# A mixture-of-experts kernel whose first piece of x is loaded ahead of the hand-synchronized section, which GpSimd enters at once and closes itself

## The chip, the cores and the metric

The kernel runs on one core of a Trainium2 chip. The metric is the device time of one execution, in microseconds; a number is the median of several runs. Besides the time, each run can leave a profile of one execution: every instruction of every engine with start and duration, the semaphore updates, and every DMA packet. The profile counts its span from the first to the last instruction of the program; the device time is longer, because it also has what lies outside the program's own instructions.

The engines are called here as the profile calls them: PE (TensorE, matrix products), PEld (its weight loads), DVE (VectorE), ACT (ScalarE), POOL (GpSimd) and SP (SyncE). A small q behind the name (SPq) means an instruction that only the engine's sequencer carries out.

## The reference

Eight experts each take 256 rows of 512 numbers through two matrix products with a ReLU in between:

```python
# x: 8 x 256 x 512, w1: 8 x 512 x 2048, w2: 8 x 2048 x 512, all float32
h = np.matmul(x, w1)
h = np.maximum(h, 0)
return np.matmul(h, w2).astype(np.float32)
```

Each weight is used for the 256 rows of one expert and never again. The weights are 2 x 33.6 MB of float32, and x and the result are 4.2 MB each.

## The kernel before

The kernel computes in bf16. Weights are read from memory as float32 and turned into bf16 by the DMA transfer itself; such casting transfers are issued by POOL, and they all stand in one queue. Each weight transfer holds one matrix of one expert (the last w2 comes in two halves) and fills one of four slots for w1 or for w2.

x goes another way at its start. Its first quarter (HEAD = 4 of 16 blocks) is loaded as float32 by SP's own queue into `x_head` and cast by DVE; POOL loads the other three quarters with the casting transfer. Both land in the third w2 slot, which is free until then. PE transposes x from there, with `identity` as the second operand, and ACT and DVE copy the transposed x from PSUM into `xT`.

Everything stands inside a critical section of Tile: in it the kernel places its own waits, and Tile only brings all engines into it and out of it again. The parts that the change touches:

```python
d_head, d_x = sem("d_head"), sem("d_x")
d_first, d_out, d_last = sem("d_first"), sem("d_out"), sem("d_last")
s_zero, s_ident, s_cast = sem("s_zero"), sem("s_ident"), sem("s_cast")
...
d_w = [sem(f"d_w{i}") for i in range(len(loads))]        # 17, one for each weight transfer

with tc.tile_critical(no_gpsimd_drain=True):             # SP is the section's own engine

    sp.dma_start(x_head[:], x_v[:, :HEAD * H]).then_inc(d_head, 16)
    for i, (w, e, h, n) in enumerate(loads):
        sp.wait_ge(d_w[i], 16)                           # a weight has landed: tell PE
        sp.sem_inc(c_w1, 1)                              # (or c_w2)
    sp.wait_ge(v_last, MC)
    sp.dma_start(out_v[:, E - 1, :], ...).then_inc(d_last, 16)   # result of the last expert

    pool.dma_start(x_sb[:, HEAD * H:], x_v[:, HEAD * H:]).then_inc(d_x, 16)
    pool.wait_ge(s_zero, 1)                              # DVE has zeroed identity
    pool.affine_select(out=identity[:], ...).then_inc(s_ident)
    for i, (w, e, h, n) in enumerate(loads):
        ...                                              # waits until the slot is free
        pool.dma_start(dst, src).then_inc(d_w[i], 16)
    pool.wait_ge(v_out, 2)
    pool.wait_ge(d_first, 16)
    pool.dma_start(out_v[:, :E - 1, :], ...).then_inc(d_out, 16) # results of experts 0 to 6
    pool.drain()

    dve.memset(identity[:], 0.0).then_inc(s_zero)
    ...
    dve.wait_ge(d_head, 16)
    dve.tensor_copy(x_sb[:, :HEAD * H], x_head[:]).then_inc(s_cast)
    ...                                                  # copies of xT and of results

    ...                                                  # ACT: copies of xT, ReLU of h
    act.wait_ge(d_out, 16)
    act.wait_ge(d_last, 16)

    pe.wait_ge(s_ident, 1)
    pe.wait_ge(s_cast, 1)
    pe.wait_ge(d_x, 16)
    loop("transposes", count, K1, transposes)
    ...
    loop("expert", count, E, expert)                     # h = x w1 by halves, then o = h w2
```

In an expert, PE waits for that expert's w1 (`c_w1`), makes h in four groups of 32 products, and then waits for w2 (`c_w2`) and makes the result.

Of the kernel before, what the change touches and what calls it, by code (L numbers as in the profile page):

```python
# [7 lines left out]

FP32 = mybir.dt.float32
BF16 = mybir.dt.bfloat16  # L10
PE = mybir.EngineType.PE

FIRST_FREE = 16512


@with_exitstack
def kernel(
# [7 lines left out]
    nc = tc.nc  # L25
    P = 128
    E, C, H = x.shape
# [7 lines left out]
    HEAD = 4  # L35

    NS = 4
# [11 lines left out]
    x_v = x.rearrange("e (pp r) k -> (e pp) (r k)", r=R)  # L49
# [4 lines left out]

    places, free = {}, FIRST_FREE

    def allot(name, shape, dtype):
        nonlocal free
        places[name] = free
        t = nc.alloc_sbuf_tensor_at(name, shape, dtype, offset=free)  # L60
        free += math.prod(shape[1:]) * mybir.dt.size(dtype)
        return t
# [3 lines left out]
    xT = allot("xT", [P, K1, MC, E * P], BF16)  # L66
    hT = allot("hT", [P, K2, C], BF16)
    out_sb = allot("out_sb", [P, E, MC, H], FP32)
    x_head = allot("x_head", [P, HEAD * H], FP32)
    identity = allot("identity", [P, P], BF16)  # L70
    W1_AT, W2_AT, XT_AT = places["w1_sb"], places["w2_sb"], places["xT"]

    x_sb = w2_sb[:, 2, :]
# [6 lines left out]
    def sem(name):  # L80
        return tc.alloc_semaphore(name)


    d_head, d_x = sem("d_head"), sem("d_x")
    d_first, d_out, d_last = sem("d_first"), sem("d_out"), sem("d_last")

    s_zero, s_ident, s_cast = sem("s_zero"), sem("s_ident"), sem("s_cast")
    p_xt, p_h, p_o = sem("p_xt"), sem("p_h"), sem("p_o")
    v_out, v_last = sem("v_out"), sem("v_last")

# [4 lines left out]
    loads = []  # L95
    for e in range(E - 1):
        loads += [(1, e, 0, 2), (2, e, 0, 2)]
    loads += [(1, E - 1, 0, 2), (2, E - 1, 0, 1), (2, E - 1, 1, 1)]
    d_w = [sem(f"d_w{i}") for i in range(len(loads))]

    with tc.tile_critical(no_gpsimd_drain=True):  # L101


        sp = nc.sync
        sp.dma_start(x_head[:], x_v[:, :HEAD * H]).then_inc(d_head, 16)
        for i, (w, e, h, n) in enumerate(loads):
            sp.wait_ge(d_w[i], 16)
            if w == 1:
                sp.sem_inc(c_w1, 1)
            else:  # L110
                sp.sem_inc(c_w2, n)
# [4 lines left out]


        pool = nc.gpsimd
        pool.dma_start(x_sb[:, HEAD * H:], x_v[:, HEAD * H:]).then_inc(d_x, 16)  # L119
        pool.wait_ge(s_zero, 1)  # L120

        pool.affine_select(  # L122
            out=identity[:],
# [7 lines left out]
        for i, (w, e, h, n) in enumerate(loads):  # L131


            old = e - NS
            if (w, e) == (2, 2):
                pool.wait_ge(p_xt, K1 * MC)
            if old >= 0 and h == 0:
                if w == 1:
                    pool.wait_ge(p_h, NG * (old + 1))
                else:  # L140
                    pool.wait_ge(p_o, MC * (old + 1))
            if i == len(loads) - 1:


                pool.wait_ge(v_out, 1)
                pool.dma_start(  # L146
                    out_v[:16, 0:5:2, :16], out_sb[:16, 0:5:2, 0, :16]
                ).then_inc(d_first, 16)
            if w == 2:
                src = w2_v[:, e, h:h + n, :].rearrange("p h n -> p (h n)")  # L150
                dst = w2_sb[:, e % NS, h * JH * H:(h + n) * JH * H]
            else:
                src, dst = w1_v[:, e, :], w1_sb[:, e % NS, :]
            pool.dma_start(dst, src).then_inc(d_w[i], 16)  # L154
        pool.wait_ge(v_out, 2)
        pool.wait_ge(d_first, 16)
        pool.dma_start(  # L157
            out_v[:, :E - 1, :], out_sb[:, :E - 1].rearrange("p e m h -> p e (m h)")
        ).then_inc(d_out, 16)
        pool.drain()  # L160

# [5 lines left out]


        dve = nc.vector
        dve.memset(identity[:], 0.0).then_inc(s_zero)  # L172
        dve.sem_inc(c_xt[0], 1)
        dve.sem_inc(c_o, MC)
        dve.wait_ge(d_head, 16)
        dve.tensor_copy(x_sb[:, :HEAD * H], x_head[:]).then_inc(s_cast)  # L176
        for ko in range(K1):
            dve.wait_ge(p_xt, ko * MC + 1)
            copy_xt(dve.tensor_copy, ko, 0).then_inc(c_xt[0])
# [11 lines left out]
        act = nc.scalar  # L191
# [14 lines left out]
                ).then_inc(c_h)  # L206
        act.wait_ge(p_o, E * MC)
        act.copy(out_sb[:, E - 1, 1, :], o_ps[1][:]).then_inc(v_last)  # L208
        act.wait_ge(d_out, 16)
        act.wait_ge(d_last, 16)  # L210

# [1 line left out]
        pe = nc.tensor  # L215
# [17 lines left out]
        def matmul(dst, weights, moving, **flags):  # L233
            inst = mybir.InstMatmult(
                name=nc.get_next_instruction_name(),
                engine=PE,
                ins=[moving, weights],
# [7 lines left out]
        def loop(name, counter, times, body):  # L245
            head, end = f"{name}_head", f"{name}_end"
            nc.br(head, engines=[PE])
            with nc.body(head, valid_engines=[PE]):
                body()
# [39 lines left out]
                    i += 1  # L289
                t.then_inc(p_xt)  # L290

        pe.wait_ge(s_ident, 1)
        pe.wait_ge(s_cast, 1)
        pe.wait_ge(d_x, 16)
        pe.reg_mov(count, 0)
        pe.reg_mov(reg["x"], X_AT + last_column(K1))
        loop("transposes", count, K1, transposes)
# [116 lines left out]
        loop("expert", count, E, expert)  # L414


# [1 line left out]
_INS = ['x', 'w1', 'w2']  # L418
_OUTS = [((8, 256, 512), 'float32')]
# [25 lines left out]
```

## Time and profile before

| what | before |
| --- | --- |
| device time, median of 3 runs | 181.04 us (181.02 to 181.25) |
| device time of the profiled run | 181.29 us |
| span of the profiled run | 179.5 us |
| PE busy | 130.4 us (73%) |
| ACT, DVE, POOL busy | 38.7, 15.9, 11.7 us |
| moved by DMA, as counted by packets | 40.37 MB, mean 225 GB/s |
| read from and written to memory | 71.30 MB and 4.20 MB |
| mean granted clock of PE | 0.961 |

The span is also shown in 40 equal slices, each about 4.5 us. A digit is a busy share in tenths, and the row DMA is the mean busy share of the core's 16 DMA engines. A stretch view gives the same for any stretch of time that is asked for: busy time of each engine, then the granted clock of PE, the busy share of the DMA engines and what they moved. A share slightly over 1 comes from packets that overlap on an engine. The timeline lists instructions by start and duration, and behind an instruction, in brackets, how long its engine had been idle and what ended that.

### The profile page before, as it was taken

What the parts mean: (1) busy time and instruction counts of PE and PEld (TensorE: products, weight loads), DVE (VectorE), ACT (ScalarE), POOL (GpSimd) and SP (SyncE); (2) the same over time, 40 slices, a digit from 0 to 9 for tenths busy, and PEclk for the clock granted to TensorE, in tenths of its full rate; (3) what the DMA queues carried; (4) which work ended last, traced back from release to release, by engine and by line L of the source; (5) the groups of instructions that cost most, each with busy time, mean ns of one, the idle gap of its engine ahead of it and who ended that gap; (6) DMA issues with size and microseconds to landing.
All of it is one profiled execution on the core that took longest, in us unless ns stands there. A gap on an engine that the chain in (4) does not pass through costs nothing. (4 is left out here: it accounts for less than half of the span.)

```text
span 179.5 us, 2103 instructions
## 1 busy us (share of the span) xinstructions
PE 130.4 (73%) x824; PEld 90.9 (51%) x832; DVE 15.9 (9%) x21; ACT 38.7 (22%) x38; POOL 11.7 (7%) x25
## 2 busy tenths in 40 slices
PE   0007659997949794949778698949894968769980
PEld 0007548746924493418633495428741963359630
DVE  0203420002000200020002000020002000200010
ACT  2002423500520044003500044003600350004410
POOL 7100030101010101010101000020000000002000
PEclk9999999999987999999999699996999999969999
DMA  5999999999999999999999999999999999999995
GB/s 186 261 203 226 230 208 204 234 215 197 230 226 212 204 230 215 197 234 226 193 223 230 208 204 234 215 197 230 226 212 204 230 215 201 230 201 211 351 423 217
DMA packets 3824, 40.37 MB, mean 225 GB/s; under 512 B 368, under 2 KB 368, under 8 KB 1392
## 3 DMA queue, kind: packets, MB, share of 16 engines
q0 software_dynamic: 3536, 38.80, 96.9%
q1 hardware_dynamic: 288, 1.57, 2.3%
HBM read 71.30 MB, written 4.20 MB: 421 GB/s over the span
## 5 line engine op out<-in xcount | busy, mean ns | idle before, releaser
L243 PE MATMUL h_ps<-xT,w_sb 128*128 x512 | 65.2, 292 | 17.1 <-PEq L218 17.1
L243 PEld LDWEIGHTS h_ps<-xT,w_sb 128*128 x512 | 59.5, 147 | 24.7 <-issue 21.7
L243 PE MATMUL o_ps<-w_sb,hT 128*128 x248 | 57.8, 387 | 11.0 <-PEq L218 10.6
L202 ACT ACTIVATE hT<-h_ps 128x1024 bf16<-128x1024 f32 x32 | 32.8, 1024 | 111.3 <-PE h_ps L243 111.3
L243 PEld LDWEIGHTS o_ps<-w_sb,hT 128*128 128x128 bf16 x256 | 24.9, 99 | 41.6 <-issue 14.0
L185 DVE COPY out_sb<-o_ps 128x512 f32<-128x512 f32 x15 | 9.7, 686 | 141.4 <-PE o_ps L243 141.4
L243 PE MATMUL xt_ps<-identity,w_sb 128*128 128x128 bf16 x64 | 7.6, 310 | 16.0 <-PEq L218 16.0
L243 PEld LDWEIGHTS xt_ps<-identity,w_sb 128*128 x64 | 6.5, 145 | 16.8 <-issue 16.8
L154 POOL DMA_DIRECT2D w_sb<-in_w_dram x17 | 9.1, 542 | 87.7 <-PE o_ps L243 34.5
L165 ACT COPY xT<-xt_ps 128x1024 bf16<-128x1024 bf16 x4 | 4.0, 1012 | 18.2 <-PE xt_ps L243 18.2
L165 DVE COPY xT<-xt_ps 128x1024 bf16<-128x1024 bf16 x4 | 4.9, 1224 | 11.9 <-PE xt_ps L243 11.9
L157 POOL DMA_DIRECT2D out_dram<-out_sb x1 | 0.9, 950 | 44.3 <-DMA out_dram<-out_sb 44.3
L208 ACT COPY out_sb<-o_ps 128x512 f32<-128x512 f32 x1 | 0.6, 586 | 5.9 <-PE o_ps L243 5.9
L146 POOL DMA_DIRECT2D out_dram<-out_sb x1 | 0.6, 557 | 20.0 <-DVEq L188 20.0
L176 DVE CAST w_sb<-x_head 128x2048 bf16<-128x2048 f32 x1 | 1.2, 1227 | 4.8 <-DMA x_head<-in_x_dram 4.8
L165 ACT ACT_TABLE_LOAD x1 | 1.3, 1283 | 1.1 <-SPq L101 1.1
L119 POOL DMA_DIRECT2D w_sb<-in_x_dram x1 | 0.7, 682 | 1.0 <-DVE identity L172 1.0
L122 POOL TENSOR_SCALAR_AFFINE_SELECT identity<-identity 128x128 bf16<-128x128 bf16 x1 | 0.3, 305 | 0.1
L172 DVE MEMSET identity<- 128x64 uint32 x1 | 0.1, 112 | 1.0 <-SPq L101 1.0
L429 POOL MEMSET const-float32-0.0<- 128x1 f32 x1 | 0.1, 99 | 0.2 <-issue 0.2
L429 POOL MEMSET const-bfloat16-1.0<- 128x1 bf16 x1 | 0.1, 102 | 0.0
L429 POOL MEMSET const-uint8-127<- 128x1 uint8 x1 | 0.1, 102 | 0.0
(1 smaller groups left out, 0.1 us busy)
## 6 DMA issues: line engine op xcount, KB each, us to landing
w_sb<-in_w_dram POOLq DMA_DIRECT2D x15, 2048.0 KB, 65.7
out_dram<-out_sb POOLq DMA_DIRECT2D x1, 3584.0 KB, 12.9
w_sb<-in_w_dram POOLq DMA_DIRECT2D x2, 1024.0 KB, 57.1
w_sb<-in_x_dram POOLq DMA_DIRECT2D x1, 1536.0 KB, 11.7
x_head<-in_x_dram SPq DMA_DIRECT2D x1, 1024.0 KB, 5.0
out_dram<-out_sb SPq DMA_DIRECT2D x1, 512.0 KB, 3.0
out_dram<-out_sb POOLq DMA_DIRECT2D x1, 3.0 KB, 44.8
```

Source lines behind the costliest of these rows:

```text
L119: pool.dma_start(x_sb[:, HEAD * H:], x_v[:, HEAD * H:]).then_inc(d_x, 16)
L122: pool.affine_select(out=identity[:], in_=identity[:], compare_op=mybir.AluOpType.not_equal, fill=1.0, base=0, pattern=[[-1, P]], channel_ ...
L146: pool.dma_start(out_v[:16, 0:5:2, :16], out_sb[:16, 0:5:2, 0, :16]).then_inc(d_first, 16)
L154: pool.dma_start(dst, src).then_inc(d_w[i], 16)
L157: pool.dma_start(out_v[:, :E - 1, :], out_sb[:, :E - 1].rearrange("p e m h -> p e (m h)")).then_inc(d_out, 16)
L165: return copy(xT[:, ko, m].rearrange("k (ep r2) -> k ep r2", r2=R // MC), xt_ps[m][:].rearrange("k r2 ep -> k ep r2"),)
L176: dve.tensor_copy(x_sb[:, :HEAD * H], x_head[:]).then_inc(s_cast)
L185: cp = dve.tensor_copy(out_sb[:, e, m, :], o_ps[m][:])
L202: act.activation(hT[:, g * GJ:(g + 1) * GJ, :].rearrange("p a c -> p (a c)"), h_ps[g % UG][:], mybir.ActivationFunctionType.Relu,).then_in ...
L208: act.copy(out_sb[:, E - 1, 1, :], o_ps[1][:]).then_inc(v_last)
L243: return pe.add_instruction(inst)
L429: nc = _bacc.Bacc("TRN2", target_bir_lowering=False, num_devices=1)
```

## The change

x_head becomes a tile of a Tile pool. Its load and its cast are moved ahead of the critical section, and Tile places the waits for them. The section is given POOL as its own engine, so that POOL takes no part in what the others wait for when they enter; only ahead of the transfer that overwrites x does it wait for Tile's data (`wait_critical_data_deps`). POOL also zeroes `identity` itself, and at the end it is POOL that waits for the two last transfers, in place of ACT. The weight transfers share one semaphore for each slot, counted up to 32, in place of one for each transfer; POOL's other transfers share one as well. The addresses of the large buffers move up by 8192 bytes a partition, since `x_head` now lies in front of them. The kernel allocates 13 semaphores fewer.

What it is for: SP and POOL are to issue the first transfers without waiting for each other, and fewer semaphores have to be cleared at the end.

```diff
-    with tc.tile_critical(no_gpsimd_drain=True):
+    landed = [
+        (d_half, 16) if h else ((d_w1, d_w2)[w - 1][e % NS], 16 * (e // NS + 1))
+        for w, e, h, _ in loads
+    ]
+    x_pool = ctx.enter_context(tc.tile_pool(name="x_pool", bufs=1))
+    x_head = x_pool.tile([P, HEAD * H], FP32, tag="x_head")
+    nc.sync.dma_start(x_head[:], x_v[:, :HEAD * H])
+    nc.vector.tensor_copy(x_sb[:, :HEAD * H], x_head[:])
+    with tc.tile_critical(sync_engine=POOL, no_gpsimd_drain=True):
...
-        sp.dma_start(x_head[:], x_v[:, :HEAD * H]).then_inc(d_head, 16)
         for i, (w, e, h, n) in enumerate(loads):
-            sp.wait_ge(d_w[i], 16)
+            sp.wait_ge(*landed[i])
...
-        pool.dma_start(x_sb[:, HEAD * H:], x_v[:, HEAD * H:]).then_inc(d_x, 16)
-        pool.wait_ge(s_zero, 1)
+        pool.dma_start(x_sb[:, HEAD * H:], x_v[:, HEAD * H:]).then_inc(d_pool, 16)
+        pool.memset(identity[:], 0.0).then_inc(s_ident)
+        pool.wait_ge(s_ident, 1)
...
             if (w, e) == (2, 2):
+                tc.wait_critical_data_deps()
                 pool.wait_ge(p_xt, K1 * MC)
...
-            pool.dma_start(dst, src).then_inc(d_w[i], 16)
+            pool.dma_start(dst, src).then_inc(landed[i][0], 16)
         pool.wait_ge(v_out, 2)
-        pool.wait_ge(d_first, 16)
+        pool.wait_ge(d_pool, 32)
         pool.dma_start(out_v[:, :E - 1, :], ...)     # the line is cut
-        ).then_inc(d_out, 16)
-        pool.drain()
+        ).then_inc(d_pool, 16)
...
-        dve.memset(identity[:], 0.0).then_inc(s_zero)
-        dve.wait_ge(d_head, 16)
-        dve.tensor_copy(x_sb[:, :HEAD * H], x_head[:]).then_inc(s_cast)
...
-        act.wait_ge(d_out, 16)
-        act.wait_ge(d_last, 16)
...
-        pe.wait_ge(s_ident, 1)
-        pe.wait_ge(s_cast, 1)
-        pe.wait_ge(d_x, 16)
+        pe.wait_ge(s_ident, 2)
+        pe.wait_ge(d_pool, 16)
...
+        pool.drain()
+        pool.wait_ge(d_pool, 48)
+        pool.wait_ge(d_last, 16).then_inc(s_ident)
```

The order in which the built program holds the instructions shows what Tile makes of it:

- SP's first instruction behind the opening barrier is now the transfer of `x_head`. Before, it was an empty instruction that raised a semaphore, and then a branch that waited for it; all engines had such a branch.
- POOL has an empty instruction in the same place, without a wait, and then its transfer of the other three quarters of x.
- SP, ACT and PE now enter the section only when the cast of x by DVE is done.
- At the end, before: all engines reported to SP, ACT after its two waits. After: POOL waits for the transfers and raises a semaphore, the other four engines answer it, and both POOL and SP wait for the answers, SP in three instructions more, before the closing barrier.
- The instruction that clears semaphores clears numbers 99 to 140 before, 42 in all, and 99 to 129 after, 31 in all, because Tile adds 8 of its own now and 6 before.

More of the change, by code (lines that the diff above doesn't have):

```diff
@@ L10 @@
 BF16 = mybir.dt.bfloat16
-PE = mybir.EngineType.PE
-FIRST_FREE = 16512
+PE, POOL = mybir.EngineType.PE, mybir.EngineType.Pool
+FIRST_FREE = 16512 + 8192
 @with_exitstack
@@ L68 @@
     out_sb = allot("out_sb", [P, E, MC, H], FP32)
-    x_head = allot("x_head", [P, HEAD * H], FP32)
     identity = allot("identity", [P, P], BF16)
@@ L81, in sem @@
         return tc.alloc_semaphore(name)
-    d_head, d_x = sem("d_head"), sem("d_x")
-    d_first, d_out, d_last = sem("d_first"), sem("d_out"), sem("d_last")
-    s_zero, s_ident, s_cast = sem("s_zero"), sem("s_ident"), sem("s_cast")
+    d_w1 = [sem(f"d_w1{i}") for i in range(NS)]
+    d_w2 = [sem(f"d_w2{i}") for i in range(NS)]
+    d_half, d_pool, d_last = sem("d_half"), sem("d_pool"), sem("d_last")
+    s_ident = sem("s_ident")
     p_xt, p_h, p_o = sem("p_xt"), sem("p_h"), sem("p_o")
@@ L98 @@
     loads += [(1, E - 1, 0, 2), (2, E - 1, 0, 1), (2, E - 1, 1, 1)]
-    d_w = [sem(f"d_w{i}") for i in range(len(loads))]
-    with tc.tile_critical(no_gpsimd_drain=True):
+    landed = [
[7 more added lines that the diff above has]
+    with tc.tile_critical(sync_engine=POOL, no_gpsimd_drain=True):
         sp = nc.sync
-        sp.dma_start(x_head[:], x_v[:, :HEAD * H]).then_inc(d_head, 16)
         for i, (w, e, h, n) in enumerate(loads):
-            sp.wait_ge(d_w[i], 16)
+            sp.wait_ge(*landed[i])
             if w == 1:
@@ L147 @@
                     out_v[:16, 0:5:2, :16], out_sb[:16, 0:5:2, 0, :16]
-                ).then_inc(d_first, 16)
+                ).then_inc(d_pool, 16)
             if w == 2:
@@ L153 @@
                 src, dst = w1_v[:, e, :], w1_sb[:, e % NS, :]
-            pool.dma_start(dst, src).then_inc(d_w[i], 16)
+            pool.dma_start(dst, src).then_inc(landed[i][0], 16)
         pool.wait_ge(v_out, 2)
-        pool.wait_ge(d_first, 16)
+        pool.wait_ge(d_pool, 32)
         pool.dma_start(
             out_v[:, :E - 1, :], out_sb[:, :E - 1].rearrange("p e m h -> p e (m h)")
-        ).then_inc(d_out, 16)
-        pool.drain()
+        ).then_inc(d_pool, 16)
         def copy_xt(copy, ko, m):
```

## The prediction, made before the changed kernel had run

> **What bounds the kernel now.** I read the slices first, because PE is busy for only 73% of the span and something else must fill it. Then I read stretches cut where the DMA row changes, then the timeline of the first 12 us, and last the chain of waits, to see whether its answer agrees.
>
> From the page:
>
> ```profile
> DMA  5999999999999999999999999999999999999995
> GB/s 186 261 203 226 230 208 204 234 215 197 230 226 212 204 230 215 197 234 226 193 223 230 208 204 234 215 197 230 226 212 204 230 215 201 230 201 211 351 423 217
> q0 software_dynamic: 3536, 38.80, 96.9%
> ```
>
> The 16 DMA engines are full in every slice but the first and the last. Nearly all of it is one queue, POOL's. The rate varies, 200 to 230 GB/s for casting transfers and 423 for plain ones, but the engines have no idle slice. The stretches show where they stand idle (after the us: five engines with busy time, granted clock, DMA share, GB/s):
>
> ```profile
> 0.00:1.90 1.90, 0.00 (x0) 0.00 (x0) 0.11 (x1) 0.84 (x1) 0.66 (x5) 1.00 0.00 0
> 1.90:2.70 0.80, 0.00 (x0) 0.00 (x0) 0.00 (x0) 0.44 (x1) 0.71 (x3) 1.00 0.90 174
> 2.70:4.80 2.10, 0.00 (x0) 0.00 (x0) 0.00 (x0) 0.00 (x0) 2.10 (x5) 1.00 0.95 394
> 13.20:158.50 145.30, 114.53 (x729) 79.95 (x736) 13.91 (x18) 32.72 (x32) 6.96 (x13) 0.96 1.01 216
> ...
> 158.50:168.20 9.70, 9.51 (x67) 8.29 (x69) 0.00 (x0) 3.66 (x4) 0.95 (x1) 0.82 1.01 227
> 168.20:175.20 7.00, 6.33 (x30) 2.66 (x28) 0.69 (x1) 1.03 (x2) 0.00 (x0) 1.00 1.02 422
> 175.20:177.90 2.70, 0.00 (x0) 0.00 (x0) 0.00 (x0) 0.00 (x0) 0.00 (x0) 1.00 0.82 335
> 177.90:179.50 1.60, 0.00 (x0) 0.00 (x0) 0.00 (x0) 0.00 (x0) 0.00 (x0) 0.84 0.00 0
> ```
>
> So the span is a start without transfers (1.9 us), transfers without a gap (176 us) and an end without transfers (1.6 us). The lone chain of waits starts at 158.59 us and follows PE to the last store. It is true that PE has no pause after the last w1 lands at 158.47, but PE is not the sole bound even there: the engines are at 1.02 until the last store is issued at 175.2, and that store's packets come behind the big store's. **Only the two ends can be shortened**, since the change moves the same bytes in the same transfers. The start is in the timeline (start, duration, engine and line, then in brackets the idle time and what ended it):
>
> ```profile
> 0.95 0.38 SPq L105 DMA_DIRECT2D x_head<-in_x_dram  x1
> 1.04 0.11 DVE L172 MEMSET identity<- 128x64 uint32 x1 [1.04 <-SPq L101]
> 1.06 1.28 ACT L165 ACT_TABLE_LOAD   x1 [1.06 <-SPq L101]
> 1.44 0.68 POOL L119 DMA_DIRECT2D w_sb<-in_x_dram  x1 [1.00 <-DVE identity L172]
> 2.22 0.30 POOL L122 TENSOR_SCALAR_AFFINE_SELECT identity<-identity 128x128 bf16<-128x128 bf16 x1
> 2.46 2.67 POOL L154 DMA_DIRECT2D w_sb<-in_w_dram  x5
> 5.93 1.23 DVE L176 CAST w_sb<-x_head 128x2048 bf16<-128x2048 f32 x1 [4.79 <-DMA x_head<-in_x_dram]
> ```
>
> The first transfer is SP's, and in the packet records its first packet runs at 1.945 us, 1.00 us after the instruction. POOL's first packet runs at 4.85 us, just as SP's packets give out. The reader is to see that **SP's instruction alone starts the DMA engines**, and that POOL has 2.7 us from its end of issue (2.13) before it is needed. The releaser that the view names for POOL, DVE's memset, is not real: POOL's wait for it stands behind the transfer in the program.
>
> **What the Trainium skill says.** "DMA: Bandwidth & Descriptors", section "Issuing engines are not separate DMA queues", says that transfers of all issuing engines share the same 16 DMA engines, so that issuing from several saves only issue time. The trace agrees: the share does not exceed 1 where both queues run. "Advanced Engine Details and Errata", section "Control Flow Timing", gives about 108 ns for a compare-and-branch. The records of SP have its branch at 0.796 us and the transfer at 0.949, 153 ns. "Runtime: NRT & Kernel Launch", on preamble and postamble, says that the runtime resets semaphores itself around every kernel. The trace shows updates on numbers 207 to 255, which the kernel does not own, at 180.2 us, behind the span; so the 1.78 us between span and device time (181.29 less 179.51) does not shrink with the kernel's own semaphores. "TensorE: Matmul & The Clock Gate", Part 1, says that PE's clock falls to half after an idle window of about 3.4 us, and that the windows run free of the kernel's start. The granted clock in the trace falls to 0.5 for 3.413 us from 158.50, which is used below.
>
> **The start, step by step.** I take pacing from the single records, since the views round them. Before, SP leaves the opening barrier at 0.661, runs the empty instruction at 0.726 and the branch at 0.796, and issues at 0.949. After, the transfer takes the place of the empty instruction: 0.949 less 0.726 is **0.22 us earlier**. Everything behind it in the saturated stretch moves by the same amount, the last w1 from 158.47 to 158.25 and the last store likewise, provided POOL's x does not come late. POOL leaves the barrier at 0.619; its next instruction stands about 0.08 behind, as its records elsewhere do, and it saves a branch of 0.15. I get 0.1 to 0.15 us earlier at 1.44. Even without any gain it would be needed only at 4.85 less 0.22, or 4.63, and it ends its issue at 2.13.
>
> What is added on POOL there is a memset of 128 columns and a wait for it. I estimate 0.2 us from the select on the same tile (0.305) and the memsets of one column (0.10). It pushes the first weight issue from 2.46 to some 2.55. That weight is behind 7 us of x in the same queue, so this costs nothing. The entry of ACT, PE and SP now waits for the cast, at about 5.7 + 1.23 = 6.9 us; ACT's table load of 1.28 us then ends near 8.3. PE's first product needs the rest of x, at 13.14 before, so this is off the path as well. The added wait ahead of the sixth weight is for the same cast and is past before the transposes are, at 23.6 us. The shared semaphores count the same events.
>
> **The end, step by step.** Before, the last store's increments are complete at 178.18. ACT wakes at 178.20, branches at 178.26, answers at 178.41; SP wakes and drains twice until 178.61; POOL passes the closing barrier's first wait at 178.637. That is 0.46 us. After, POOL wakes at 0.02 and, at its pace of 0.078 for each instruction, raises the section's semaphore at 0.10, passes its empty instruction at 0.18, two waits at 0.26 and 0.33, another empty instruction at 0.41, a drain at 0.49 and the barrier's wait at 0.57. SP, in parallel, gets the answers at 0.17 (DVE answered 0.056 us after such a raise, in the records at 175.6) and needs three waits and two drains of 0.06, until about 0.47. So POOL's own row sets the end: 0.57 in place of 0.46, **0.11 us later**.
>
> Then comes the clearing:
>
> ```profile
> L440 POOLq EVENT_SEMAPHORE_RANGE_CLEAR  x1: 266/266/266, 178.9 to 178.9; - x1
> ```
>
> Its 42 updates run from 178.970 to 179.187, 5.2 ns each. Eleven fewer save **0.06 us**. POOL's drain moves behind the section's other code but not in POOL's own order; it lasted until 177.82 before, with 0.36 us to spare to 178.18, and moves along with the store.
>
> The sum is -0.22 + 0.11 - 0.06 = -0.17 us, and 181.04 - 0.17 = **180.87 us**.
>
> **The rivals.** First, the clock. The last expert starts at half clock:
>
> ```profile
> 138.90:143.10 4.20, 3.87 (x34) 3.72 (x35) 0.00 (x0) 1.17 (x2) 0.00 (x0) 1.00 1.02 218
> 158.30:162.50 4.20, 3.86 (x21) 3.22 (x22) 0.00 (x0) 0.26 (x1) 0.00 (x0) 0.59 1.04 217
> ```
>
> The expert before did 34 products in such a stretch, this one 21. Over the 3.413 us at half clock PE loses 1.7 us. If another phase of the window spared it this, PE would end near 173.0 and the last store would be issued at 173.6. If PE bounded the end, the time would be about 179.4. But the DMA engines are full until about 177.3 with the same bytes, and an earlier store can only fill the 0.18 idle share of the 2.7 us after 175.2: at most 0.5 us. The four known times, 181.02 to 181.29, speak against large swings. I leave this for the low end.
>
> Second, a new wait at the start. If SP's transfer paid the cost of entering a new block, or if POOL's packets came only just in time at 4.85, the gain would be 0.1 or none, and with the longer end the time would be 181.0 to 181.1. For it speaks that POOL's packets begin exactly when SP's end; against it, that all sixteen engines change over without a gap though they finish SP's part 0.7 us apart.
>
> Third, the end outweighs the start: the extra round through all engines costs 0.3 us rather than 0.11, if SP's three waits run one after another and not beside POOL's. That makes 181.05. Fourth, the moved buffers: an offset of 8192 bytes could change the rate of the transfers, where 1% would be 1.7 us. Nothing in the trace speaks for it.
>
> **Range and chances.** The two ends each carry some 0.1 us of doubt, the three runs before lie 0.23 apart, and the clock may take some off. That gives 180.55 to 181.15. Two per cent are 3.6 us, more than both idle ends of the DMA engines together (3.5 us), so I put 0.98 on within 2%.
>
> **What would show it.** Right, if SP's first transfer starts near 0.73 and the first packet near 1.73, if the weights land 0.2 us earlier each with the same 9.7 us between them, and if the end of the span is 1.35 to 1.4 us behind the last landing, 1.33 before. Wrong, if an idle gap appears near 4.6 us, if the landings drift apart, or if the clear is not shorter by 0.06. A time below 180.4 would mean that the granted clock of the last expert matters more than I allow.

## The result and the profile after

The changed kernel takes 181.97 us (median of 6 runs, 181.84 to 182.04), the kernel before 181.06 (6 runs): a ratio of 1.0047, with a 95% interval of 1.0034 to 1.006. It is slower by about 0.9 us. The range was 180.55 to 181.15.

The span did not grow: it is 179.2 us in the profiled run, before 179.5. So I split each time into two: the **span**, and the **outside part**, which is the device time of a run less the span of the same run. Before, the outside part was 1.78 us (181.29 less 179.51); after, it is 2.81 (182.04 less 179.23), and 2.45 to 2.84 over the six runs, median 2.61. By the medians 0.83 of the 0.91 us are there, and the span's median is 179.35 us, that of the kernel before 179.3 to 179.4 (in the runs beside the experiments).

First the inside, which the prediction spoke of. These are the stretches of the changed kernel, cut as those of before, each shifted with the work (five engines with busy time and number of instructions, granted clock, DMA share, GB/s):

```profile
0.00:1.70 1.70, 0.00 (x0) 0.00 (x0) 0.00 (x0) 0.00 (x0) 0.60 (x5) 1.00 0.00 0
1.70:2.50 0.80, 0.00 (x0) 0.00 (x0) 0.00 (x0) 0.00 (x0) 0.56 (x3) 1.00 1.00 195
2.50:4.60 2.10, 0.00 (x0) 0.00 (x0) 0.00 (x0) 0.00 (x0) 1.96 (x5) 1.00 0.99 412
4.60:12.80 8.20, 0.00 (x0) 0.00 (x0) 1.23 (x1) 1.28 (x1) 0.95 (x2) 1.00 1.06 227
12.80:158.10 145.30, 115.72 (x729) 79.14 (x736) 13.92 (x18) 32.72 (x32) 6.97 (x13) 0.95 1.01 216
158.10:167.80 9.70, 9.53 (x74) 8.09 (x76) 0.00 (x0) 4.10 (x4) 0.95 (x1) 1.00 1.00 222
167.80:174.80 7.00, 4.75 (x22) 1.96 (x20) 0.69 (x1) 0.59 (x1) 0.00 (x0) 1.00 1.02 421
174.80:177.50 2.70, 0.00 (x0) 0.00 (x0) 0.00 (x0) 0.00 (x0) 0.00 (x0) 1.00 0.88 358
177.50:179.20 1.70, 0.00 (x0) 0.00 (x0) 0.00 (x0) 0.00 (x0) 0.00 (x0) 0.63 0.00 0
```

The shape is that of before, 0.2 us earlier: nothing until 1.7, the DMA engines full from there, nothing behind 177.5. There is no gap at 4.6, where POOL's transfer takes over from SP's: in the packet records POOL's first packets start at 4.59 us, and SP's last ones end at 5.11. The timeline of the start:

```profile
0.74 0.38 SPq L110 DMA_DIRECT2D x_head<-in_x_dram  x1
1.31 0.68 POOL L128 DMA_DIRECT2D w_sb<-in_x_dram  x1 [0.86 <-POOLq L438]
1.99 0.22 POOL L129 MEMSET identity<- 128x128 bf16 x1
2.45 0.28 POOL L132 TENSOR_SCALAR_AFFINE_SELECT identity<-identity 128x128 bf16<-128x128 bf16 x1 [0.24 <-POOL identity L129]
2.87 2.68 POOL L165 DMA_DIRECT2D w_sb<-in_w_dram  x5
5.52 1.23 DVE L111 CAST w_sb<-x_head 128x2048 bf16<-128x2048 f32 x1 [5.52 <-DMA x_head<-in_x_dram]
7.07 1.28 ACT L175 ACT_TABLE_LOAD   x1 [7.07 <-DVE w_sb L111]
```

SP issues at 0.74 in place of 0.95 and POOL at 1.31 in place of 1.44. The first packet runs at 1.75 in place of 1.95. The first weight is issued 0.4 us later than before (2.87) and ACT's table load 6 us later (7.07); neither delays a landing. The weights land 0.37 to 0.42 us earlier than in the profile of before (the last w1 at 158.05 in place of 158.47). The clear of the semaphores at the end:

```profile
L449 POOLq EVENT_SEMAPHORE_RANGE_CLEAR  x1: 203/203/203, 178.7 to 178.7; - x1
```

It lasts 203 ns, before 266.

Now the outside. The DMA view of the changed kernel for the stretch from 179 to 184 us, behind the span, has one packet (count, MB, share):

```profile
DMA packets 1, 0.02 MB, mean 3 GB/s; under 512 B 0, under 2 KB 0, under 8 KB 0
...
q8 instruction: 1, 0.02, 1.6%
```

The same view of the kernel before, behind its span:

```profile
DMA packets 0, 0.00 MB, mean 0 GB/s; under 512 B 0, under 2 KB 0, under 8 KB 0
```

**The reader is to see the kind of the packet: instruction.** Its record says 16384 bytes, from 180.96 to 182.28 us, so it ends 3.05 us behind the span. Some engine fetches a block of program after the kernel has ended, while the runtime's closing code runs. The updates of semaphores behind the span tell who may be waiting. The runtime resets semaphores 3 to 255 there, in five groups that start at different times. Four groups start 0.01, 0.66, 0.77 and 0.82 us behind the span in both kernels. The fifth, numbers 3 to 53, starts at 0.98 us before and at 1.26 after. Semaphore 2 is changed 18 times behind the span, step after step; I call that the closing round. Its steps behind the resets come 0.27 us later than before, the last two 0.38. The last one stands at 2.29 us in place of 1.91, so most of the 1.03 us that this run's outside part has more lies behind the last update on record.

### The profile page after: what moved, and what is told of

Read it like the earlier page. It is cut to its first block, busy times and chain, and to the rows that moved or that the text cites. A ratio compares the mean times of both kernels' runs of the same rounds, so it can differ in the third digit from the quotient of the medians.

```text
span 179.2 us, 2110 instructions
## 1 busy us (share of the span) xinstructions
PE 130.0 (73%) x824; PEld 89.2 (50%) x832; DVE 15.8 (9%) x20; ACT 38.7 (22%) x38; POOL 12.0 (7%) x26
## 5 line engine op out<-in xcount | busy, mean ns | idle before, releaser
L248 PE MATMUL o_ps<-w_sb,hT 128*128 x248 | 62.4, 409 | 14.6 <-PEq L223 13.8
L248 PE MATMUL h_ps<-xT,w_sb 128*128 x512 | 60.2, 277 | 12.3 <-PEq L223 12.3
L248 PEld LDWEIGHTS h_ps<-xT,w_sb 128*128 x512 | 56.6, 145 | 17.9 <-issue 17.1
L248 PEld LDWEIGHTS o_ps<-w_sb,hT 128*128 128x128 bf16 x256 | 26.1, 104 | 48.6 <-issue 24.0
```

Of the source, the lines that this page charges most:

```text
L248: return pe.add_instruction(inst)
```

## The experiments

All have the whole computation. Counts of instructions are those of the built program, loops counted once, unless records are named: POOL 47 before and 56 after, PE 128 and 129. In the table, time, span and outside part are medians in us over a kernel's runs, and the ratio is to the kernel before on the same chip.

| kernel | changed in it | time | span | outside | ratio (95%) |
| --- | --- | --- | --- | --- | --- |
| after | - | 181.97 | 179.35 | 2.61 | 1.0047 (1.0034 to 1.006) |
| b_pool9 | before, POOL +9 | 181.13 | 179.35 | 1.79 | 1.0006 (0.9997 to 1.0014) |
| b_pool4 | before, POOL +4 | 181.13 | 179.35 | 1.79 | 1.0003 (0.9995 to 1.0012) |
| b_pe1 | before, PE +1 at its start | 182.08 | 179.35 | 2.68 | 1.005 (1.0033 to 1.0066) |
| b_sems | before, shared semaphores | 181.09 | 179.3 | 1.76 | 0.9998 (0.9987 to 1.0008) |
| b_others9 | before, ACT, DVE, SP +9 each | 181.1 | 179.3 | 1.79 | 0.9994 (0.998 to 1.0008) |
| b_pe1_tail | before, PE +1 at its end | 181.65 | 179.35 | 2.29 | 1.0024 (1.0007 to 1.004) |
| a_pe1less | after, PE -1 | 181.4 | 179.5 | 1.94 | 1.0029 (1.0012 to 1.0047) |
| a_sp_close | the same, SP closes | 180.81 | 178.9 | 1.91 | 0.9986 (0.9975 to 0.9996) |
| a_sp_act1 | the same, ACT +1 | 180.68 | 178.9 | 1.76 | 0.9978 (0.9967 to 0.9988) |
| a_pe_act | after, PE -1, ACT +1 | 181.3 | 179.5 | 1.79 | 1.0013 (0.9994 to 1.0033) |
| b_act1less | before, ACT -1 | 181.22 | 179.25 | 1.96 | 1.0005 (0.9987 to 1.0024) |
| b_pe8 | before, PE +8 | 182.09 | 180.3 | 1.78 | 1.0051 (1.0029 to 1.0074) |
| b_pe3 | before, PE +3 | 182.13 | 179.4 | 2.55 | 1.0053 (1.0039 to 1.0067) |
| b_pe16 | before, PE +16 | 182.03 | 180.3 | 1.8 | 1.0043 (1.0031 to 1.0055) |
| a_pe16 | after, PE +16 | 182.12 | 180.2 | 1.94 | 1.0055 (1.0038 to 1.0071) |

The kernel before, run beside them, had median spans of 179.3 to 179.4 and outside parts of 1.76 to 1.79 throughout.

### Whose program is too long: b_pool9, b_pool4, b_pe1

My first theory was POOL, whose program grew most. In b_pool9, and with four in b_pool4:

```diff
+        for _ in range(9):
+            pool.sem_inc(s_zero, 1)
         pool.wait_ge(v_out, 2)
```

> The kernel before, with nine more instructions on POOL and nothing else: nine raises of the spent semaphore s_zero, where POOL idles ahead of the store of experts 0 to 6, so that POOL has 56 instructions in the program, as in the changed kernel (47 before). Theory A (the changed kernel's time went into one 16 KB instruction fetch behind the span, at 180.96 us, because POOL's longer program moves the runtime's closing code across a block of instructions): the time rises from 181.06 to 181.9 to 182.1, the span stays at 179.5, and an instruction packet of 16384 bytes on queue 8 shows near 181 us. Theory B (PE's one instruction more moves PE's closing code across a block): no change, 181.0 to 181.2, no such packet. Theory C (that POOL closes the section leaves something for the runtime to finish): no change either.

> The same with four instructions more on POOL, 51 in all. Theory A puts the edge somewhere between 48 and 56 instructions and does not say where; so the time is either 181.06 with no packet on queue 8, or the full 181.9 to 182.1 with it, and nothing between. A cost that grew with each instruction would give about 181.45. Theories B and C: 181.06.

Neither moved: 181.13 us, outside 1.79, no packet behind the span. The theory fell. The rival theory was PE's one instruction more:

```diff
+        pe.sem_inc(s_zero, 1)
         pe.reg_mov(count, 0)
```

> The kernel before with one raise of s_zero more on PE, ahead of the transposes: PE has 129 instructions, as in the changed kernel, and POOL stays at 47. Theory A: 181.06, no packet on queue 8. Theory B: 181.9 to 182.1 with the packet. Theory C: 181.06.

One instruction of PE, a single raise of a spent semaphore at 13 us, made 182.08 us of 181.11. The span is that of before, the outside part 2.68. The DMA view behind the span of b_pe1:

```profile
DMA packets 2, 0.02 MB, mean 5 GB/s; under 512 B 0, under 2 KB 0, under 8 KB 0
...
q8 instruction: 1, 0.02, 1.9%
q14 instruction: 1, 0.01, 0.4%
```

The packet on queue 8 is there again (181.13 us, 16384 bytes), and the resets of numbers 3 to 53 start 1.26 us behind the span, as in the changed kernel. So one instruction more on PE does it, without any other part of the change.

### The rest of the change alone: b_sems, b_others9

b_sems takes the shared semaphores only (32 cleared, 42 before):

```diff
-    d_w = [sem(f"d_w{i}") for i in range(len(loads))]
+    landed = [
+        (d_half, 16) if h else ((d_w1, d_w2)[w - 1][e % NS], 16 * (e // NS + 1))
+        for w, e, h, _ in loads
+    ]
...
```

> The kernel before with the shared semaphores alone: one for each weight slot and one for POOL's other transfers; x_head, the entry and the end stay as they were. 32 semaphores are cleared in place of 42 and each engine has as many instructions as before. All theories: the clear shortens by 10 x 5.2 ns to about 0.21 us and the time by 0.05 us, to 181.0. If the number of the kernel's semaphores changed what the runtime does behind the span, the time would differ by more.

The clear fell from 266 to 204 ns and the part from the last landing to the end of the span from 1.33 to 1.25 us in the profiled run. The time, 181.09, does not resolve it; the outside part, 1.76, is not touched by the number of semaphores.

b_others9 is the control for the other engines:

```diff
+    s_spare = sem("s_spare")
...
         act.sem_inc(c_h, UG)
+        for eng in (nc.scalar, nc.vector, nc.sync):
+            for _ in range(9):
+                eng.sem_inc(s_spare, 1)
```

> The kernel before with nine more raises of an otherwise unused semaphore on each of ACT, DVE and SP, where they idle at the start (ACT 69, DVE 46, SP 46 instructions; PE stays at 128, POOL at 47). If only PE stands at the edge of a block: 181.1, nothing on queue 8. If any engine's added instructions cost something outside the span, 181.3 or more.

181.1 us, outside 1.79, nothing on queue 8. But there is a fetch, a shorter one on queue 14 (from 179.2 us on):

```profile
DMA packets 1, 0.01 MB, mean 2 GB/s; under 512 B 0, under 2 KB 0, under 8 KB 0
...
q14 instruction: 1, 0.01, 0.4%
```

Its record says 8192 bytes, from 179.38 to 179.69 us. It ends 0.35 us behind the span, long before the closing round does (1.91), and costs nothing. A fetch behind the span is thus not a loss in itself; it has to end late.

### Taking PE's instruction out of the changed kernel: a_pe1less, and adding it elsewhere: b_pe1_tail

```diff
-        act.sem_inc(c_h, UG)
+        act.sem_inc(c_h, UG - 1)
...
-        take(c_h, 1)
         loop("expert", count, E, expert)
```

> The changed kernel with one instruction less on PE: ACT starts the count of free h buffers at one in place of two, and PE's first decrement of it, ahead of the experts, is left out. PE has 128 instructions, as in the kernel before. If PE's one instruction more is the whole loss, the fetch on queue 8 is gone, the part outside the span falls from 2.81 us back to 1.78, and the sum of measured parts is: first packet at 1.75, 176.05 from there to the last landing, 1.44 of exit, 1.78 outside, 181.0 us in all, 0.1 under the kernel before (181.1). If closing the section on POOL, or the other part of the change, costs time outside the span too, it stays above 181.3.

The fetch is gone. The DMA view behind the span of a_pe1less:

```profile
DMA packets 0, 0.00 MB, mean 0 GB/s; under 512 B 0, under 2 KB 0, under 8 KB 0
```

The outside part fell from 2.61 to 1.94, in all 22 runs between 1.89 and 1.98. That is 0.67 of the 0.83 us; 0.16 stayed, which the next experiments take up. The time did not come out as expected, 181.4, because the spans scattered from 179.1 to 181.0. A scatter is seen in every kernel measured beside it, but here 11 of 22 spans are at 179.6 or more, in the kernel before 16 of 67.

In b_pe1_tail the instruction stands behind the last expert:

```diff
         loop("expert", count, E, expert)
+        pe.sem_inc(s_zero, 1)
```

> The kernel before with one raise of s_zero more on PE, this time behind the last expert. If the length of PE's program up to the closing code is what counts, it costs the same as the one ahead of the transposes: 182.0 to 182.2 with a 16384 byte packet on queue 8. If the wait or the raise at PE's start was what mattered in b_pe1, it stays at 181.1.

It costs 0.5 us outside (2.29), less than at PE's start, and the profiled run has no packet on queue 8 but one of 8192 bytes on queue 14 at 181.45 us. So one instruction more costs in both places, and the place has some say. Why another and shorter packet is fetched here stays open. That it is the end of the fetch that counts is seen in the four profiled runs that have a late one (us behind the span; b_pe3 is told below):

| kernel | fetch ends | outside part of this run | difference |
| --- | --- | --- | --- |
| after | 3.05 | 2.81 | 0.24 |
| b_pe1 | 3.18 | 2.94 | 0.24 |
| b_pe3 | 2.75 | 2.51 | 0.24 |
| b_pe1_tail | 2.68 | 2.43 | 0.25 |

The fetches last from 0.55 to 1.45 us, and the device time ends with each of them, 0.24 to 0.25 us ahead of its last byte on the profile's time scale.

### The other 0.16 us, and the end: a_sp_close, a_sp_act1, b_act1less, a_pe_act

a_sp_close is a_pe1less with SP closing the section:

```diff
-    with tc.tile_critical(sync_engine=POOL, no_gpsimd_drain=True):
+    with tc.tile_critical(no_gpsimd_drain=True):
```

> The kernel a_pe1less, but SP closes the section, as before the change; POOL still enters without a wait, because its wait for Tile's data stands in the middle of its program, and POOL still waits for the last two transfers. The round through all engines at the end falls away: from the last landing POOL wakes at 0.02, answers at 0.10, SP passes at 0.14 and drains until 0.25, so that POOL passes the closing barrier's first wait at about 0.3 us in place of 0.64 in the changed kernel. Sum: 1.75 + 176.05 + 1.10 + 1.78 = 180.7 us. If the cost of the end lies in the waits and not in the round, it stays at 181.0. If POOL's entry depends on who closes, its transfer of x starts near 7 us and the time rises by 2 us or more.

The closing barrier's first wait passes 0.34 us behind the last landing (0.64 in the changed kernel, 0.46 before), and the span is 178.9. POOL still issues its x at 1.23 us. The time is 180.81; the 0.1 us above the expected 180.7 is again the outside part of 1.91. That is nearly the 1.94 of a_pe1less, so which engine closes the section matters inside the span and not outside.

In the changed kernel, a_pe1less and a_sp_close one step of the closing round on semaphore 2 took 0.15 us in place of 0.034. ACT has 56 instructions in the records of these and 57 before: its two waits at the end are gone, one at its entry is new. (The built programs do not show this, ACT has 60 in both; they also hold branches that leave no record.) So a_sp_act1 gives a_sp_close one more, and b_act1less takes one from the kernel before:

```diff
+    s_spare = sem("s_spare")
...
         act.sem_inc(c_h, UG - 1)
+        act.sem_inc(s_spare, 1)
```

And b_act1less, where DVE does what ACT did:

```diff
         dve.sem_inc(c_xt[0], 1)
+        dve.sem_inc(c_xt[1], 1)
...
-        act.sem_inc(c_xt[1], 1)
```

> The kernel a_sp_close with one instruction more on ACT, a raise of an unused semaphore, so that ACT carries out 57 instructions as in the kernel before (56 in the changed kernel, a_pe1less and a_sp_close). In those three the part outside the span held 0.12 us more at one step of the closing round of semaphore 2. If this comes from ACT's program being one shorter, the outside part falls from 1.92 to 1.78 and the time from 180.81 to 180.67. If it comes from what POOL, SP or DVE carry out, or from the entry through Tile, it stays at 1.92 and 180.8.

> The kernel before with ACT one instruction shorter: its raise of c_xt[1] is done by DVE. If the step of 0.12 us follows ACT's length, the outside part rises from 1.78 to 1.9 and the time to 181.2. If not, 181.1.

Both came as expected, in opposite directions: adding an instruction to ACT took the outside part from 1.91 to 1.76, removing one raised it from 1.77 to 1.96, 1.89 to 1.98 in all 12 runs. The step is back to 0.034 us in the first and 0.146 in the second. a_sp_act1, 180.68 us, is faster than both kernels: 0.9978 of the kernel before, 0.9967 to 0.9988. Its start and end:

```profile
0.74 0.38 SPq L111 DMA_DIRECT2D x_head<-in_x_dram  x1
1.23 0.68 POOL L129 DMA_DIRECT2D w_sb<-in_x_dram  x1 [0.78 <-POOLq L439]
```

```profile
L450 POOLq EVENT_SEMAPHORE_RANGE_CLEAR  x1: 204/204/204, 178.4 to 178.4; - x1
```

The first fence is the timeline, the second the view of the line that closes the program. The start is that of the changed kernel, and the clear comes at 178.4 us in place of 178.7.

a_pe_act keeps POOL as the closing engine and mends PE and ACT:

> The changed kernel with PE one instruction shorter (as in a_pe1less) and ACT one longer, nothing else: POOL still closes the section. If the whole loss of the changed kernel is the place of the closing code of PE and of ACT, the outside part is 1.78 and the span stays at 179.2: 181.0 us, 0.1 under the kernel before. If the scattered spans of a_pe1less (179.1 to 181.0) belong to that kernel and not to its chip, they come back here.

The outside part is 1.79, the whole loss is out of it. The time of 181.3 is not clear of the kernel before, and no gain is shown for the change itself: seven of 14 spans are at 179.6 or more. With a_pe1less that makes 18 of 36, in the kernel before, run beside them, 26 of 112, in a_sp_close and a_sp_act1 5 of 44. In its profiled run (span 180.7) one of the 16 DMA engines landed x at 13.73 us, the others by 12.80; one packet at 5.50 us took 1619 ns where its kind takes 926. What held it isn't in the records, nor why these two kernels scatter more.

### A longer program of PE: b_pe8, b_pe3, b_pe16, a_pe16

The edit is that of b_pe1 with 8, 3 and 16 raises, and 16 in the changed kernel.

> The kernel before with eight more raises on PE ahead of the transposes, 136 instructions. If the loss is one fetch at a block's edge, it is the same as with one: outside 2.4 to 2.9 us, 181.9 to 182.1 in all. If it grows with each instruction, 185 or more. If only certain places are bad, it may be back at 181.1.

> The kernel before with three raises of s_zero more on PE ahead of the transposes, 131 instructions. If the edge of a block lies in PE's closing code and the first instructions behind it are missing when they are needed: the outside part is over 2.2 us as with one (2.45 to 2.93), with a packet of 16384 bytes on queue 8 near 181 us. If only the one place of b_pe1 is bad: 1.78 and 181.1.

> The kernel before with sixteen raises of s_zero more on PE ahead of the transposes, 144 instructions. If the edge has moved ahead, into code that PE passes while it has time (it waits from about 174 us for the last store), the fetch stands before 178 us, the outside part is 1.78, the span 179.3 and the time 181.1. If a longer program always pays for the fetch, inside or outside of the span, it is 181.9 or more.

> The changed kernel with sixteen raises of an unused semaphore more on PE ahead of the transposes; all else is the changed kernel, ACT's shorter program too. If its loss is only where the edge falls, the outside part is 1.93 (with ACT's 0.15), the span 179.3 and the time 181.2, in place of 181.97. If a longer program pays as well, 182 or more.

b_pe3 is b_pe1 again (outside 2.55, fetch at 181.44 us). With 8, 16 and 16 the outside part is that of before (1.94 with ACT's 0.16 in a_pe16), but **the time stays at 182.0 to 182.1, since the span has grown to 180.2 or 180.3**. I had hoped to move the edge between two blocks of program to a place where the fetch is free; it wasn't.

In b_pe16 the fetch stands within the span. The DMA view of 41.4 to 42.6 us:

```profile
q0 software_dynamic: 23, 0.25, 97.6%
q8 instruction: 1, 0.02, 4.9%
```

One packet of 16 KB holds one DMA engine for 944 ns (4.9% of 16 engines in 1.2 us), while the others carry weights. By the landings, the weight under way then took 11.16 us and the next 9.06, together 0.84 more than twice the usual 9.69.

A landing is 16 increments of a semaphore. For the weights up to 32.41 us they come within 0.6 us; for the weight under way at the fetch the last one is 1.4 us behind the other fifteen, and 0.8 us at every later weight (62.31 after 61.48, 164.03 after 163.21). The increments name no engine, but this is what one engine looks like that has lost the time of the fetch and doesn't win it back; each weight is complete only when that engine is done. So a fetch in the middle delays the stream, in this run by nearly all that the span has grown.

In a_pe16 x was late by 1.0 us already, on two of the 16 engines, and its fetch at 43.7 us put a third beside them: two increments come late at 42.85 us, three at 52.49. No landing moved, since it was late already; what held x isn't known. In b_pe8 the fetch ran at 177.81, and the profiled run lost at most 0.3 us by it: its last store landed 1.49 us behind the big store, elsewhere 1.20 to 1.25. The other five runs of b_pe8 took 0.5 to 1.4 us longer, and no profile tells why.

## Why the prediction was wrong

**What bounds it: right.** The DMA engines do. From the first packet to the last landing it is 176.04 us after and 176.23 before. The clock was the test of it. In the changed kernel's profile the last expert ran at full speed:

```profile
157.90:162.10 4.20, 3.88 (x34) 3.72 (x35) 0.00 (x0) 1.18 (x2) 0.00 (x0) 1.00 1.03 217
```

It did 34 products in a stretch where it had done 21 before, and the last store was issued at 173.19 us, 2.0 earlier. The DMA issues on the two pages, after and before, show where that went:

```profile
out_dram<-out_sb SPq DMA_DIRECT2D x1, 512.0 KB, 4.6
```

```profile
out_dram<-out_sb SPq DMA_DIRECT2D x1, 512.0 KB, 3.0
```

The last number is the time to landing: 1.6 of the 2.0 us went into a longer wait in the DMA engines, and 0.4 is left, about half of it the earlier start. So the first rival was rightly kept small. PE's half clock came for 3.413 us, as the prediction says, but not after 3.4 us of idling: PE had been idle for 2.5 us at 158.50, and in the first 13 us, in which it does nothing, its clock stands at 1.00. Another reading doesn't hold: the DMA share does exceed 1 where both queues run, it is 1.43 between 4.8 and 5.6 us before. At the end, from 175.2 to 176.6, it is 1.00.

**The start: right.** Expected 0.73 and 1.73 for SP's issue and the first packet, measured 0.74 and 1.75; POOL's issue was expected at 1.29 to 1.34 and is at 1.31. POOL's memset takes 0.224, its wait another 0.24; the first weight is 0.4 later in place of 0.1, hidden as argued. Only the landings came earlier than forecast, by 0.4 us in place of 0.2. The other 0.2 is the shorter stream (176.04 in place of 176.23), which is chance: b_pool9, b_pool4, b_sems, b_others9 and b_pe1 have the start of before, and 176.02 to 176.11.

**The end: right in kind, too small.** Expected 0.57 from the last landing to the barrier, measured 0.64 (before 0.46), and to the end of the span 1.44 in place of 1.35 to 1.4. POOL's instructions that wait for two semaphores are 0.09 us apart and not 0.078. The clear is shorter by 0.063, expected 0.06. Start, end and clear give -0.20 + 0.18 - 0.06 = -0.08 in place of -0.17; these parts are a gain inside the span, about half of what I worked out, and too small for the medians of the spans to show.

**The outside part: this step failed.** The prediction took 1.78 us over unchanged, with the argument that the runtime resets semaphores that the kernel doesn't own. That argument is right (b_sems, 1.76). But it spoke of semaphores alone and never asked what else of the kernel reaches into the closing code. The instructions on PE and on ACT do: one more on PE and one fewer on ACT cost time there, while nine more on POOL, or on ACT, DVE and SP together, changed nothing. I had the order of the instructions of both kernels and had read that the other engines enter behind the cast; I did not count that this wait for three semaphores needs one instruction more on PE. The missing term is +0.83 (2.61 less 1.78): 0.67 from PE, as a_pe1less shows, and 0.16 from ACT, as b_act1less and a_sp_act1 show. With it the sum is 181.06 - 0.08 + 0.83 = 181.8, and 181.97 was measured; the other 0.16 isn't accounted for.

The Trainium skill has the block: "Runtime: NRT & Kernel Launch", section "Instruction fetch mechanics", says that instructions are refilled in blocks of 16 KiB, 256 instructions, and that crossing an edge is "mostly hidden". The packets of 16384 bytes agree; those of 8192 bytes it doesn't have. The early fetch of b_others9 was hidden, the late ones were not: these cost 0.7 to 0.9 us of the outside part with 1 and 3 instructions more on PE. With 16 more, within the span, it was 0.8 by the landings of b_pe16. No record names the engine that queue 8 serves; that it is PE's program follows from the fetch coming, moving and going with PE's count.

## What to carry to other kernels

Where a change is worth tenths of a microsecond, count the instructions of each engine before and after, and compare device time less span as well as the span. A single instruction more, here on PE, can cost more than all the waits that it helps to remove. And when the DMA engines are full from the first packet to the last, only the two ends count: move the first issue forward, and let the engine that closes be one that needs no extra round, as in a_sp_act1.

## What the runs showed of the hardware

- One instruction more on PE, 129 in place of 128 in the built program, brought a fetch of 16384 bytes behind the span (1.32 us long in the changed kernel, 1.45 in b_pe1), and 0.67 us (the changed kernel against a_pe1less) to 0.89 us (b_pe1) of the outside part.
- The end of such a fetch set the end of the device time: in four profiled runs the two are 0.24 to 0.25 us apart. A fetch that ended 0.35 us behind the span (b_others9) cost nothing.
- In b_pe16 a fetch of 944 ns held one of 16 busy DMA engines, and its share of every later weight came 0.8 us behind the others'.
- One instruction less in ACT's records (56 in place of 57) lengthened one step of the runtime's closing round from 0.034 to 0.146 us (b_act1less), and one more took it back (a_sp_act1). What it is in ACT's stream that pays for this isn't known.
- Clearing 42 semaphores took 266 ns, 32 took 204 and 31 took 203: about 6 ns for each one fewer.
- PE's half-clock stretches of 3.413 us fell elsewhere in each profile; the last one ahead of the last store began at 158.5 us before and at 130.1 after. The last store was issued 2.0 us earlier without it in the last expert, and landed 0.4 us earlier.
